# Gate/up feature tiles as seven half products: eight tiles more, raw weights in pairs, evictions in place

## The chip, the cores and the metric

The kernel runs on one core of a Trainium2 chip. The metric is device time in microseconds (us) of one execution. TensorE (PE in the rows, PEld for its weight loads) multiplies, VectorE (DVE) and ScalarE (ACT) do elementwise work, GpSimd (POOL) does a little of it, and SyncE (SP) issues the transfers from HBM. PSUM is the accumulator memory: eight banks of 128 partitions by 512 float32, called B0 to B7 here.

## The reference, cut to what matters

Two layers, each a token mixer (state space heads, stick-breaking attention, block-sparse attention) and a SwiGLU feed-forward part, on 512 tokens of width 1024 in float32. The change lies in the feed-forward part, hidden width 2816:

```
h2 = rms_norm(x, pre_ffn_norm)
f = (jax.nn.silu(h2 @ w_gate) * (h2 @ w_up)) @ w_down
return x + rms_norm(f, post_ffn_norm)
```

`rms_norm(x, w)` is `x * rsqrt(mean(x*x) + 1e-6) * w`, over the width.

## The kernel before, in words

**Two-part numbers.** Every float32 operand of a matmul is split into a high part `hi`, which ScalarE writes (a copy that rounds, L114), and a low part `lo = src - hi`, which VectorE writes (L115). A product is three matmuls: hi by hi, hi by lo, lo by hi (`PASSES`). So each weight tile of 128x1024 costs a transfer of 512 KB by SyncE into a raw slot (`wr0` to `wr2`, a ring of three), a copy of ScalarE into one of four `wh`, and a subtraction of VectorE into one of four `wl`. `chunk` does that for a whole tile (L128 is its transfer).

**The stages of a layer.** Input projections and the mixer; the output projection (L561), in whose end each token tile's post-norm and pre-norm stand (`post_norm` L193 to L197, `pre_norm` L184 to L187, then PE transposes L170 and `to_hT`, which writes the transposed activations hi and lo into `hT` and keeps an unsplit copy, L176); gate/up; down (L685). The stages follow one another with no barrier: the weights of the next stage are fetched and split while the last one multiplies.

**Gate/up.** There are 22 feature tiles of 128 in a layer. Two forms compute one.
- `plain`: gate and up each take 24 matmuls of 128x512 (all 512 tokens; L218 in `fm_mm`): 48. Six tiles, 0, 1, 5, 9, 13 and 17 (`PLAIN`), go this way; 0 and 1 do it by token halves, since the last tokens' norms are still under way.
- `seven`: the other 16. The activations are cut into 2 by 2 blocks (token halves by width halves), and so are the weights: `b11`, `b21` are the two halves of the gate tile, `b12`, `b22` those of the up tile. Seven products of blocks and sums of blocks, in the manner of Strassen and Winograd, take the place of eight: 7 products of 12 matmuls of 128x256 (L619), 84. The sums on the activations' side (`XS`, three in the tiles `D`, one in `RR0` and `RR1`) are made once per layer (L598 to L601). Those on the weights' side are made per tile by VectorE: `t13` holds `b11+b12` and `b12+b22`, `t24` holds `b11+b12+b22` and that plus `b21`; they use `RR2` and `RR3` as scratch.

**A seven tile on the engines.** VectorE does the weight sums (L644, L645, L647, L649), five `lo` subtractions (two of 128x1024, for w0 and w13, and three of 128x512, for the halves of w24 and for w22), and seven operations of 128x256 that combine the products (L658 to L671). ScalarE does the `hi` copies, a copy of the first product out of PSUM (L656) and two silus (L153). The results stand in eight slots `F0` to `F3` (`take_ct`, four per tile), and in the tile `GT[i]`.

**What sets the order.** A scheduler orders each engine's instructions by priorities. The weight work stands under `high_priority(SPLIT_OFF)`, so that it comes ahead of the combining operations where it can. Each engine runs its list strictly in order: an instruction that waits holds all those behind it. A slot of a ring can be filled again only when the last reader of its former content is done.

**Down.** The 22 tiles of `GT` are split into hi and lo again, into the four tiles of `RR` in rotation, hi in one half and lo in the other (`R = cut(RR)`: `RR0` first), and multiplied (L685) into all eight PSUM banks.

## Time and profile before

| | |
|---|---|
| median of 3 runs | 1249.36 us (1248.89 to 1250.68) |
| profiled execution | 1248.79 us; span of its instructions 1247.0 us |
| PE busy | 1214.4 us (97%) |
| DVE, ACT, POOL busy | 825.5 (66%), 590.3 (47%), 54.0 (4%) us |
| granted PE clock, mean over the span | 0.995 of full speed |
| gate/up, layer 0 | 270.12 to 505.51 us (first L218 to first L685) |
| gate/up, layer 1 | 887.11 to 1120.08 us |

Times of rows are in us from the start of the span. The matmuls are pipelined: one of 128x256 is listed with 283 ns, but they start 120 ns apart, so the cost of a matmul is read from a run of them (duration of the run by its count), not from one. The same holds in a smaller way on VectorE and ScalarE, where a next operation can start before the listed end of the last.

### The profile page before, as it was taken

The page shows a single profiled execution, that of the slowest core. Times are in us where ns is not written, and L with a number is a line of the kernel's source. Part 1 is how long each engine was busy: PE and PEld are TensorE (multiplying, and loading weights), DVE is VectorE, ACT ScalarE, POOL GpSimd, SP SyncE. Part 2 cuts the span into 40 slices and gives each one's busy share as a digit, 9 for nine tenths or more (in the row PEclk, how much of TensorE's full clock was granted, in tenths as well). Part 3 has the DMA queues.
Part 4 walks back from the last instruction along what each step waited for, and adds up shares of the span by engine and source line. Part 5 has one row for each costly group of instructions (what it writes and reads, how often), then busy time and mean ns, then how long its engine had stood idle before and what let it go on. Part 6 is the DMA issues. An engine that isn't in the chain of part 4 may idle for free.

```text
span 1247.0 us, 18442 instructions
## 1 busy us (share of the span) xinstructions
PE 1214.4 (97%) x7270; PEld 1074.4 (86%) x7270; DVE 825.5 (66%) x1459; ACT 590.3 (47%) x1084; POOL 54.0 (4%) x88
## 2 busy tenths in 40 slices
PE   6999999999999999899999999999999999999997
PEld 5877888889999999788877888888899999998886
DVE  5466866889777768433465578578897778683334
ACT  5555664465444444422355566635654444353232
POOL 1010000110000000000010100001000000000000
PEclk9999999999999999999999999999999999999999
DMA  7332233242333333333324322221423323334321
GB/s 243 119 96 74 85 102 102 69 152 68 105 116 96 108 102 117 120 101 98 105 85 135 120 70 83 77 94 68 153 70 103 116 92 108 106 107 131 92 77 68
DMA packets 40775, 128.90 MB, mean 103 GB/s; under 512 B 5456, under 2 KB 5744, under 8 KB 40688
## 3 DMA queue, kind: packets, MB, share of 16 engines
q1 hardware_dynamic: 39344, 123.49, 30.9%
q0 software_dynamic: 1344, 4.23, 1.0%
q8 instruction: 57, 0.93, 0.3%
q14 instruction: 30, 0.25, 0.1%
HBM read 123.47 MB, written 4.23 MB: 102 GB/s over the span
## 4 chain that ended last, share of the span: by engine, by line
PE 91%; DVE 3%; ACT 2%; issue 1%; DMA 1%; SPq 0%; DVEq 0%; POOLq 0%; POOL 0%; ACTq 0%
PE B L218 24%; PE B L619 23%; PE B L685 19%; PE B L209 7%; PE B L561 7%; PE B L336 2%; PE B L343 1%; PE B L449 1%; PE B L314 1%; DMA wr<-in_wch_dram 1%; PE B L170 1%; PE B L521 1%; PE B L315 1%; DVE wl L115 1%; ACT wh L114 1%
## 5 line engine op out<-in xcount | busy, mean ns | idle before, releaser
L218 PE MATMUL B<-hT,wh 128*128 128x512 f32 (+1 forms) x1024 | 296.6, 370 | 2.2 <-ACT F L303 2.2
L115 DVE TENSOR_TENSOR wl<-wr,wh 128x1024 fp32r<-128x1024 f32 (+1 forms) x204 | 230.5, 1137 | 84.2 <-ACT wh L114 82.2
L114 ACT ACTIVATE wh<-wr 128x1024 fp32r<-128x1024 f32 (+1 forms) x204 | 200.4, 989 | 129.6 <-DMA wr<-in_wch_dram 40.1
L218 PEld LDWEIGHTS B<-hT,wh 128*128 128x128 f32 x1024 | 184.7, 191 | 31.6 <-ACT F L303 3.3
L685 PE MATMUL B<-wh,RR 128*128 128x512 f32 x704 | 189.8, 389 | 3.9 <-ACT RR L114 3.9
L218 PE MATMUL B<-hT,wl 128*128 128x512 f32 (+1 forms) x512 | 188.2, 369 | 0.0
L685 PEld LDWEIGHTS B<-wh,RR 128*128 128x128 f32 x704 | 132.0, 188 | 31.6 <-ACT RR L114 4.3
L619 PE MATMUL B<-hT,wh 128*128 128x256 f32 x768 | 152.1, 283 | 0.9 <-ACT F L656 0.9
L619 PE MATMUL B<-D,wh 128*128 128x256 f32 x768 | 148.9, 283 | 0.0
L619 PEld LDWEIGHTS B<-hT,wh 128*128 128x128 f32 x768 | 125.5, 192 | 1.5 <-ACT F L656 1.4
L619 PEld LDWEIGHTS B<-D,wh 128*128 128x128 f32 x768 | 123.9, 192 | 0.4
L114 ACT ACTIVATE wh<-RR 128x512 fp32r<-128x512 f32 (+1 forms) x96 | 73.9, 774 | 97.7 <-PE B L619 42.5
L685 PE MATMUL B<-wl,RR 128*128 128x512 f32 x352 | 109.5, 389 | 0.0
L218 PEld LDWEIGHTS B<-hT,wl 128*128 128x128 f32 x512 | 97.7, 191 | 13.7
L619 PE MATMUL B<-hT,wl 128*128 128x256 f32 x384 | 108.7, 283 | 0.0
L619 PE MATMUL B<-D,wl 128*128 128x256 f32 x384 | 107.8, 283 | 0.0
L115 DVE TENSOR_TENSOR RR<-F,RR 128x512 fp32r<-128x512 f32 x48 | 33.1, 691 | 111.3 <-ACT RR L114 110.6
L115 DVE TENSOR_TENSOR wl<-RR,wh 128x512 fp32r<-128x512 f32 (+1 forms) x96 | 82.5, 863 | 17.7 <-ACT wh L114 17.2
L114 ACT ACTIVATE RR<-F 128x512 fp32r<-128x512 f32 x48 | 30.0, 629 | 131.2 <-PE B L685 130.8
L209 PE MATMUL B<-wh,hT 128*128 128x512 f32 x256 | 84.1, 404 | 2.4 <-DVE hT L115 2.4
L685 PEld LDWEIGHTS B<-wl,RR 128*128 128x128 f32 x352 | 66.1, 188 | 13.7
L561 PE MATMUL B<-wh,RR 128*128 128x512 f32 x256 | 77.2, 398 | 0.0
(190 smaller groups left out, 1869.1 us busy)
## 6 DMA issues: line engine op xcount, KB each, us to landing
wr<-in_wch_dram SPq DMA_DIRECT2D x204, 512.0 KB, 3.6
x<-in_x_dram SPq DMA_DIRECT2D x16, 256.0 KB, 3.4
F<-in_gains_dram SPq DMA_DIRECT2D x16, 256.0 KB, 4.1
F<-acd POOLq DMA_DIRECT2D x16, 256.0 KB, 6.2
xsave<-x SPq DMA_DIRECT2D x8, 256.0 KB, 2.1
x<-xsave SPq DMA_DIRECT2D x8, 256.0 KB, 3.4
out_dram<-x SPq DMA_DIRECT2D x8, 256.0 KB, 2.0
D<-in_mixgain_dram SPq DMA_DIRECT2D x4, 256.0 KB, 4.9
```

Of the source, the lines that this page charges most:

```text
L114: A.activation(hi, src, AF.Copy)
L115: return eng.tensor_tensor(lo, src, hi.bitcast(F32), op=OP.subtract)
L170: T.transpose(p[:, i * P:(i + 1) * P], srcs[q + i], ident)
L209: T.matmul(p, hT[a][:, k, t * P:(t + 1) * P], w[k // 2][b][:, (k % 2) * 512:(k % 2 + 1) * 512], start=n == 0, stop=n == 3 * KT - 1)
L218: T.matmul(p[:, t0 * P:t1 * P], w[b][:, k * P:(k + 1) * P], hT[a][:, k, t0 * P:t1 * P], start=first and n == 0, stop=n == 3 * KT - 1, skip ...
L314: T.matmul(p, tiles[2 + h][:, cs], tiles[h][:, cd], start=True, stop=False, skip_group_check=True)
L315: T.matmul(p, tiles[2 + h][:, cs], tiles[4 + h][:, cd], start=False, stop=stop, skip_group_check=True)
L336: T.matmul(pz[:, o:w], ntri if i2 == i else nones, s2, start=False, stop=i2 == NT - 1 and n == 1, skip_group_check=True)
L343: T.matmul(pv[:, j * 64:(j + 1) * 64], e[:, (j - i) * P:(j - i + 1) * P], VT[i][:, h * 64:(h + 1) * 64], start=i == NT - 1, stop=i == 0 an ...
L561: T.matmul(OB[j][hf], lt, w[b][:, hf * 512:(hf + 1) * 512], start=k == ks[0] and a == 0 and b == 0, stop=k == ks[-1] and a == 1)
L619: T.matmul(p, w[b][:, half * 512 + k * P:half * 512 + (k + 1) * P], left(j, a, k), start=first and k == 0 and n == 0, stop=k == 3 and n == ...
L685: T.matmul(B[2 * t + hf], gs[a][:, t * P:(t + 1) * P], w[b][:, hf * 512:(hf + 1) * 512], start=i == 0 and a == 0 and b == 0, stop=i == HT ...
```

## The change

- `PLAIN` becomes `(0, 1)`: tiles 5, 9, 13 and 17 are computed as seven half products too, 20 of 22 in each layer.
- The raw weights lie in one tensor `WRT` of four slots of 128x1024. The first three are the ring of `chunk`. The fourth is also the norms' scratch `F[43:45]`. `seven` takes slots in pairs: 0 and 1, or 2 and 3.
- `t13` is made in one VectorE operation of 128x1024 (L648: `b11` and `b22` by a stride, `b12` broadcast over both) where two of 128x512 stood (L644, L647).
- The products are combined in place: the silus write into their PSUM banks (`pa`, `pd`), the subtraction of `wv` from `pd` as well; the two multiplications read one operand from PSUM. A tile takes two slots of `F0`, `F1`, not four of `F0` to `F3`; the silu of plain tiles uses `F2`, `F3`.
- `to_hT` splits first and keeps the copy after.
- `down` begins its rotation with `RR2` and `RR3`.

Lines move by two to four: L115 becomes L117, L619 L622, L644 L648, L645 L650, L649 L653, L656 L660, L658 to L671 L662 to L675, L685 L689.

```diff
-PLAIN = (0, 1, 5, 9, 13, 17)
+PLAIN = (0, 1)
...
-    WR = [cp.tile([P, D], F32, name=f"wr{i}") for i in range(NRAW)]
+    WRT = cp.tile([P, NRAW + 1, D], F32, name="wr")
+    WR = [WRT[:, i] for i in range(NRAW)]
+    F[43:45] = [WRT[:, NRAW, h * 512:(h + 1) * 512] for h in range(2)]
...
         def dst(q, n, p):
+            sl = slice(t * P, (t + 1) * P)
+            split(p.rearrange("p (k l) -> p k l", k=4), hT[0][:, q:q + n, sl], hT[1][:, q:q + n, sl])
             if keep is not None:
                 A.activation(keep[q // 4], p, AF.Copy)
-            sl = slice(t * P, (t + 1) * P)
-            split(p.rearrange("p (k l) -> p k l", k=4), hT[0][:, q:q + n, sl], hT[1][:, q:q + n, sl])
...
-        take_sg = ring(F[43:45])
-        take_ct = ring([f[:, h * 256:(h + 1) * 256] for f in F[0:4] for h in range(2)])
+        take_sg = ring(F[2:4])
+        take_ct = ring([f[:, h * 256:(h + 1) * 256] for f in F[0:2] for h in range(2)])
+        take_pair = ring([WRT[:, 0:2], WRT[:, 2:4]])
...
-            rg, ru = take_raw(), take_raw()
-            b11, b21, b12, b22 = rg[:, lo5], rg[:, hi5], ru[:, lo5], ru[:, hi5]
-            for n, r in enumerate((rg, ru)):
-                nc.sync.dma_start(r, wch[l, C_GU + 2 * i + n])
+            raw = take_pair()
+            for n in range(2):
+                nc.sync.dma_start(raw[:, n], wch[l, C_GU + 2 * i + n])
+            rg, raw4 = raw[:, 0], raw.rearrange("p a (h n) -> p (a h) n", h=2)
+            b21, b22 = raw4[:, 1], raw4[:, 3]
...
-                V.tensor_tensor(t13[:, lo5], b11, b12, op=OP.add)
+                V.tensor_tensor(t13.rearrange("p (h n) -> p h n", h=2), raw4[:, 0:4:3],
+                                raw4[:, 2:3].to_broadcast([P, 2, 512]), op=OP.add)
                 V.tensor_tensor(t24[:, lo5], t13[:, lo5], b22, op=OP.add)
                 split(t24[:, lo5], w24[0][:, lo5], w24[1][:, lo5])
-                V.tensor_tensor(t13[:, hi5], b12, b22, op=OP.add)
...
-            wv, xv, uv, sg = take_ct(), take_ct(), take_ct(), take_ct()
+            wv, xv = take_ct(), take_ct()
...
-            silu(sg, pa)
+            silu(pa, pa)
             product(pd, w24, 1, 2, False)
-            V.tensor_tensor(uv, pd, wv, op=OP.subtract)
-            silu(uv, uv)
-            V.tensor_tensor(t1, xv, uv, op=OP.mult)
+            V.tensor_tensor(pd, pd, wv, op=OP.subtract)
+            silu(pd, pd)
+            V.tensor_tensor(t1, pd, xv, op=OP.mult)
             product(pc, w22, 0, 6, False)
             V.tensor_tensor(wv, wv, pc, op=OP.subtract)
-            V.tensor_tensor(t0, wv, sg, op=OP.mult)
+            V.tensor_tensor(t0, pa, wv, op=OP.mult)
...
-        R = cut(RR)
+        R = cut(RR[2:4] + RR[0:2])
```

Three places of the program show how instructions move. The number behind a name tells which allocation it is; B0 to B7 are PSUM banks, wl and wh the split weights, wr the raw slots.

**The start of gate/up, layer 0, on VectorE.** L197 or L199 ends a token's post-norm (token tile 3's here), L187 or L189 is the pre-norm of token tiles 2 and 3, L644 or L648 the first weight sum of feature tile 2. Before:

```order
L644 TENSOR_TENSOR RR2_2162<-wr1_107,wr2_108 128x512
L647 TENSOR_TENSOR RR2_2162<-wr2_108 128x512
L197 SCALAR_TENSOR_TENSOR x30_1243<-F2_65,SM_117,x30_1243 128x512
L197 SCALAR_TENSOR_TENSOR x31_1244<-F3_66,SM_117,x31_1244 128x512
L160 TENSOR_SCALAR SM_117<-SM_117 128x1
L645 TENSOR_TENSOR RR3_2163<-RR2_2162,wr2_108 128x512
L160 TENSOR_SCALAR SM_117<-SM_117 128x1
L187 SCALAR_TENSOR_TENSOR F0_63<-x20_1241,SM_117,F20_73 128x512
L187 SCALAR_TENSOR_TENSOR F1_64<-x21_1242,SM_117,F21_74 128x512
L649 TENSOR_TENSOR RR3_2163<-RR3_2163,wr1_107 128x512
L187 SCALAR_TENSOR_TENSOR F43_84<-x30_1243,SM_117,F20_73 128x512
L187 SCALAR_TENSOR_TENSOR F44_85<-x31_1244,SM_117,F21_74 128x512
```

Now the same stretch reads:

```order
L117 TENSOR_TENSOR wl3_112<-wr_104,wh3_108 128x1024
L162 TENSOR_SCALAR SM_113<-SM_113 128x1
L199 SCALAR_TENSOR_TENSOR x30_1239<-F2_65,SM_113,x30_1239 128x512
L199 SCALAR_TENSOR_TENSOR x31_1240<-F3_66,SM_113,x31_1240 128x512
L189 SCALAR_TENSOR_TENSOR F0_63<-x20_1237,SM_113,F20_73 128x512
L189 SCALAR_TENSOR_TENSOR F1_64<-x21_1238,SM_113,F21_74 128x512
L162 TENSOR_SCALAR SM_113<-SM_113 128x1
L648 TENSOR_TENSOR RR2_2158<-wr_104 128x1024
L189 SCALAR_TENSOR_TENSOR wr_104<-x30_1239,SM_113,F20_73 128x512
L189 SCALAR_TENSOR_TENSOR wr_104<-x31_1240,SM_113,F21_74 128x512
L650 TENSOR_TENSOR RR3_2159<-RR2_2158,wr_104 128x512
L117 TENSOR_TENSOR hT1_95<-B1_97,hT0_94 128x4x128
```

The weight sum moved behind token tile 2's pre-norm and stands right ahead of token tile 3's, whose scratch is now the fourth raw slot.

**The steady state of gate/up, layer 0, on VectorE.** Twelve rows in a row, from the weight sum of one tile on. L666, L668, L670 and L671 are the last four combining operations of a tile (L670, L672, L674 and L675 now), L658 to L662 the first three (L662 to L666 now). Before:

```order
L644 TENSOR_TENSOR RR2_2162<-wr1_107,wr2_108 128x512
L647 TENSOR_TENSOR RR2_2162<-wr2_108 128x512
L645 TENSOR_TENSOR RR3_2163<-RR2_2162,wr2_108 128x512
L658 TENSOR_TENSOR F0_63<-B4_102,F0_63 128x256
L649 TENSOR_TENSOR RR3_2163<-RR3_2163,wr1_107 128x512
L660 TENSOR_TENSOR F0_63<-F0_63,B3_101 128x256
L115 TENSOR_TENSOR wl3_116<-RR3_2163,wh3_112 128x512
L662 TENSOR_TENSOR F0_63<-F0_63,B1_99 128x256
L115 TENSOR_TENSOR wl0_113<-RR2_2162,wh0_109 128x1024
L115 TENSOR_TENSOR wl2_115<-wr1_107,wh2_111 128x1024
L666 TENSOR_TENSOR F1_64<-B3_101,F0_63 128x256
L115 TENSOR_TENSOR wl3_116<-RR3_2163,wh3_112 128x512
```

Now:

```order
L117 TENSOR_TENSOR wl2_111<-RR2_2158,wh2_107 128x1024
L117 TENSOR_TENSOR wl0_109<-wr_104,wh0_105 128x1024
L648 TENSOR_TENSOR RR2_2158<-wr_104 128x1024
L670 TENSOR_TENSOR B3_99<-B3_99,F0_63 128x256
L117 TENSOR_TENSOR wl1_110<-RR3_2159,wh1_106 128x512
L650 TENSOR_TENSOR RR3_2159<-RR2_2158,wr_104 128x512
L674 TENSOR_TENSOR F0_63<-F0_63,B1_97 128x256
L117 TENSOR_TENSOR wl3_112<-wr_104,wh3_108 128x512
L672 TENSOR_TENSOR F18_1231<-B3_99,F0_63 128x256
L653 TENSOR_TENSOR RR3_2159<-RR3_2159,wr_104 128x512
L675 TENSOR_TENSOR F18_1231<-B2_98,F0_63 128x256
L117 TENSOR_TENSOR wl1_110<-RR3_2159,wh1_106 128x512
```

L648 takes the place of L644 and L647, and it stands ahead of the last four combining operations of the tile that PE is finishing; those write or read PSUM now (`B3`, `B2`), where `F1` stood.

**The end of gate/up and the start of down, layer 0, on ScalarE.** F12 to F15 are the first four results of gate/up, that down splits into RR; L153 (L155 now) is the silu. Before:

```order
L656 ACTIVATE F2_65<-B5_103 128x256
L114 ACTIVATE wh2_111<-wr1_107 128x1024
L114 ACTIVATE wh0_109<-wr2_108 128x1024
L153 ACTIVATE F3_66<-B5_103 128x256
L114 ACTIVATE wh1_110<-wr0_106 128x1024
L153 ACTIVATE F3_66<-F3_66 128x256
L144 ACT_TABLE_LOAD
L114 ACTIVATE RR0_4380<-F12_67 128x512
L114 ACTIVATE RR1_4381<-F13_68 128x512
```

Now:

```order
L116 ACTIVATE RR2_4574<-F12_67 128x512
L116 ACTIVATE wh1_106<-RR3_2159 128x512
L155 ACTIVATE B3_99<-B3_99 128x256
L116 ACTIVATE wh3_108<-wr_104 128x512
L116 ACTIVATE RR3_4575<-F13_68 128x512
L660 ACTIVATE F1_64<-B5_101 128x256
L116 ACTIVATE wh2_107<-wr_104 128x1024
L116 ACTIVATE wh0_105<-wr_104 128x1024
L155 ACTIVATE B5_101<-B5_101 128x256
L116 ACTIVATE wh1_106<-wr_104 128x1024
L116 ACTIVATE RR0_4572<-F14_69 128x512
L116 ACTIVATE RR1_4573<-F15_70 128x512
```

The split of F12, the first that down's matmuls read, moved from behind the last silu and the table load to the middle of the last feature tile.

## Rows read from the trace of the kernel before

**Rows 1.** Page, section 1: busy us, share of the span, instructions.

```profile
PE 1214.4 (97%) x7270; PEld 1074.4 (86%) x7270; DVE 825.5 (66%) x1459; ACT 590.3 (47%) x1084; POOL 54.0 (4%) x88
```

**Rows 2.** PE's waits, 255 to 630 us: line, releaser: us, times, longest.

```profile
PE B L685 <- ACT RR L114: 3.1, 1, 3.1
...
PE B L170 <- DVE hT L115: 1.6, 1, 1.6
PE B L619 <- ACT F L656: 0.5, 1, 0.5
```

**Rows 3.** PE's waits, 870 to 1247 us (L170 and L619 as in rows 2).

```profile
PE B L685 <- ACT RR L114: 0.8, 1, 0.8
```

**Rows 4.** Chain that ended last: start, us, engine, line, count.

```profile
270.12 11.51 PE B L218 x96
...
409.97 10.95 PE B L218 x48
...
452.60 10.91 PE B L218 x48
463.51 37.45 PE B L619 x312
...
505.51 116.79 PE B L685 x514
...
887.11 11.51 PE B L218 x96
...
1120.08 115.68 PE B L685 x509
```

**Rows 5.** Windows: stretch, length, busy us by engine, clock, DMA share, GB/s.

```profile
463.50:501.00 37.50, 37.50 (x315) 37.50 (x314) 31.39 (x55) 18.21 (x30) 0.00 (x0) 1.00 0.32 99
```

**Rows 6.** DVE by line and form, 255 to 520 us: busy us, mean ns.

```profile
L115 DVE TENSOR_TENSOR wl<-wr,wh 128x1024 fp32r<-128x1024 f32 x38 | 45.9, 1220 | 14.2 <-ACT wh L114 14.0
...
L668 DVE TENSOR_TENSOR F<-F,F 128x256 f32<-128x256 f32 x16 | 6.7, 418 | 0.0
...
L660 DVE TENSOR_TENSOR F<-F,B 128x256 f32<-128x256 f32 x16 | 6.6, 415 | 2.6 <-PE B L619 2.1
```

**Rows 7.** Timeline of DVE, layer 0: start us, us, instruction.

```profile
467.23 0.68 DVE L645 TENSOR_TENSOR RR<-RR,wr 128x512 f32<-128x512 f32 x1
467.84 1.21 DVE L115 TENSOR_TENSOR wl<-wr,wh 128x1024 fp32r<-128x1024 f32 x1
468.97 0.41 DVE L660 TENSOR_TENSOR F<-F,B 128x256 f32<-128x256 f32 x1
469.30 0.68 DVE L649 TENSOR_TENSOR RR<-RR,wr 128x512 f32<-128x512 f32 x1
```

**Rows 8.** ACT by line and form, 255 to 520 us.

```profile
L153 ACT ACTIVATE F<-F 128x256 f32<-128x256 f32 x16 | 6.6, 413 | 4.9 <-DVE F L666 4.9
...
L153 ACT ACTIVATE F<-B 128x256 f32<-128x256 f32 x16 | 5.8, 365 | 0.0
```

**Rows 9.** L639, the transfers of seven tiles: waiters (us, times), landing times.

```profile
  DVE RR L644: 19.4, 24
...
DMA to landing us min/median/max: 3.3/3.6/5.3
```

**Rows 10.** Timeline at the end of gate/up, layer 0.

```profile
499.98 2.01 ACT L114 ACTIVATE wh<-wr 128x1024 fp32r<-128x1024 f32 x2 [3.30 <-DMA wr<-in_wch_dram]
...
504.82 1.15 ACT L114 ACTIVATE RR<-F 128x512 fp32r<-128x512 f32 x2
```

**Rows 11.** Timeline of ACT at the end of gate/up, layer 1.

```profile
1115.98 2.01 ACT L114 ACTIVATE wh<-wr 128x1024 fp32r<-128x1024 f32 x2 [2.36 <-DMA wr<-in_wch_dram]
```

**Rows 12.** Timeline of DVE at the start of gate/up, layer 0.

```profile
280.68 1.41 DVE L187 SCALAR_TENSOR_TENSOR F<-x,SM,F 128x512 f32<-128x512 f32 x2
282.74 0.69 DVE L600 TENSOR_TENSOR F<-F,F 128x512 f32<-128x512 f32 x1 [0.65 <-ACT F L176]
```

More of the change, by code (lines that the diff above doesn't have):

```diff
@@ L71, in cut @@
         return [t[:, h * 512:(h + 1) * 512] for t in tiles for h in range(2)]
-    F = [None if 4 <= i < 12 or 18 <= i < 20 or 28 <= i < 40 else cp.tile([P, 512], F32, name=f"F{i}")
+    F = [None if 4 <= i < 12 or 18 <= i < 20 or 28 <= i < 40 or i >= 43 else cp.tile([P, 512], F32, name=f"F{i}")
          for i in range(NF)]
```

## The prediction

> **What bounds the kernel now.** The page's busy shares come first: PE is busy for 97% of the span, DVE for 66%, ACT for 47% [rows 1]. So nearly all of the time is the matmuls' own, and the kernel can gain in two ways only: fewer or cheaper matmuls, or the few us in which PE waits. PE's waits in the two stretches that the change touches are 3.1 us at down's first matmul in layer 0 and 0.8 us in layer 1, 0.5 us in either layer at the first seven tile, and 1.6 us in the transposes ahead of gate/up [rows 2, 3]. Between those waits the chain that ended last consists of PE runs alone: a plain tile is 48 matmuls in 10.91 to 10.95 us, and 312 matmuls of 128x256 take 37.45 us [rows 4]. The window over that second run shows PE busy for all of its 37.50 us, DVE for 31.39 and ACT for 18.21, with the clock at 1.00 [rows 5]. So in gate/up PE sets the pace, DVE follows at 84%, and what a tile costs is its number of matmuls by their spacing, as long as DVE keeps up.
>
> **The change part by part.**
>
> *Four plain tiles per layer become sevens.* The run of sevens gives 37.45 / 312 = 0.120 us a matmul, so a tile of 84 takes 10.08 us. A plain tile takes 10.93 (the middle of 10.91 and 10.95) [rows 4]. That is 0.85 us less per tile, 6.8 us for eight. It is all on PE's path.
>
> These rows also price size: a 128x512 matmul takes 10.93 / 48 = 0.228 us, two of 128x256 take 0.240, so halving the width costs 5%. The Trainium skill (Perfetto Trace Analysis, Optimizing Tensor Performance, Matmuls) says that larger matmuls are more efficient than smaller ones, which speaks against the change. The rows agree with it, and the 6.8 us has that price in it: by columns alone (84x256 against 48x512, 12.5% fewer) a tile would save 1.37 us, and eight 10.9.
>
> *DVE's work per seven tile.* In the timeline the next operation starts 0.61 us after one of 128x512, 1.13 after one of 128x1024 and 0.33 after one of 128x256 [rows 7]. Before, a tile is two of 1024 columns, seven of 512 and seven of 256: 2x1.13 + 7x0.61 + 7x0.33 = 8.84. With the fused `t13` it is three, five and seven: 3x1.13 + 5x0.61 + 7x0.33 = 8.75. Against PE's 10.08 DVE has 1.33 us free per tile (87% full). Before, plain tiles gave it more rest: they need little of DVE, and a seven behind one could run ahead. Now 20 sevens follow one another, so this 1.33 us has to suffice each time. It does if no single wait in DVE's queue is longer.
>
> *In place in PSUM.* Three of DVE's 256-column operations change where an operand or the result lies: two multiplications read one operand from PSUM, and the subtraction `pd - wv` writes its result there. Reading is shown: 415 ns with a PSUM operand (L660), 418 with both in SBUF (L668) [rows 6]. Writing PSUM from DVE or ACT no row shows. The bounds: nothing, or even a gain, as ACT's silu takes 365 ns when it reads PSUM and 413 when it reads SBUF [rows 8]; and at the other end as much again as the operation (0.42 us for one DVE operation and 0.37 for each of two silus). I take nothing, the nearest rows being L660 and L668. At the upper end DVE would need 8.75 + 0.42 = 9.17 of 10.08, and ACT has half its time free, so PE would not notice.
>
> The Trainium skill gives a fixed cost per DVE operation of about 60 ns on SBUF and 125 ns on PSUM (Perfetto Trace Analysis, Optimizing Scalar/DVE Operations). As an estimate from that page three operations would cost 3 x 65 = 0.2 us more per tile, and the sum would stay as it is, with the free time of DVE down to 1.1 us. L660 against L668 shows no such difference here.
>
> *Raw weights in pairs.* The gate and up tiles of a feature tile now land in one of two pairs instead of three single slots in rotation. A transfer takes 3.6 us from issue to landing (3.3 to 5.3), and DVE's first weight sum waited for one 24 times, 19.4 us in all [rows 9], without PE waiting for it. A pair is free when the last split that reads it (w22's `lo`) is done. Laying the order of DVE, ACT and PE out by the spacings above, layer 0 issues the up transfer of tile i+2 at 2.0 us into a period of 10.08, it lands at 5.6. DVE ends L666 at about 4.85 (it waits for the fourth product of the tile), `wl2` follows ACT's `wh2` until 6.75 and `wl0` ACT's `wh0` until 8.3, where DVE comes to L648: 2.7 us to spare. In layer 1 the order is another, L648 stands ahead of more: the transfer lands at 6.8 and DVE comes to it at 6.9. There PE has some 1.3 us of weights in hand behind it. So up to a landing of 3.6 + 1.3 = 4.9 us costs nothing, and each us above that is lost 1:1 in that tile. Only landings near the slowest seen (5.3) would be felt, at 0.4 us. I take nothing for both layers; if one in five of layer 1's twenty landed that late, 4 x 0.4 = 1.6 us.
>
> *The start.* The first seven is tile 2. Its gate transfer can only be issued when the first pair is free, that is when tile 1's up weights are split. L648 for tile 2 now waits for it, and stands on DVE ahead of token 3's pre-norm, with the transposes and the first matmuls on token 3 behind that. Before, that pre-norm ran from 280.68 to about 282.1 [rows 12]. By the timeline of before tile 1's up split ends at about 276.2, the transfer lands at 276.2 + 3.6 = 279.8, and L648 (1.13) is followed by the pre-norm until 282.3, so 0.2 to 0.3 us late in layer 0. The transposes of token 2 have moved in among tile 1's matmuls, so that PE has work there, and the 0.5 us wait for L656 at the first seven [rows 2, 3] should go. I take 0.6 us gained in layer 0, between -1 (landing at 5.3 instead of 3.6, less 0.7 covered) and 1.1. In layer 1 the same chain is about 0.85 us later at token 3, and tile 3's split of w0 may be late by 0.65: against the 0.5 won I take nothing, between -0.7 and 0.5.
>
> *to_hT.* The copy that is kept follows the split instead of preceding it, so hT is ready some 0.5 us sooner, and the bank is freed at the same time as before, after three operations on two engines. The 1.6 us wait of the transposes for that bank [rows 2] stays. I cost it at nothing.
>
> *The end.* Before, down's first split had to wait for the last product, since RR0 held one of its operands; it also stood on ACT behind two raw copies that had waited 3.30 us for their transfer, the last silu and a table load, and so began at 504.82, with PE's first down matmul at 505.51 [rows 4, 10]. In the new order that split stands in the last feature tile, into RR2, free after the last weight sum. Then the first down weights (ACT `wh0`, DVE `wl0`) are due last, 8.2 to 8.3 us into the 8.64 that PE spends on the last tile after its second product has gone ahead (72 x 0.120): in time. The 3.1 us [rows 2] go. In layer 1 the copy of a down weight, which waited 2.36 us for its transfer before [rows 11], stands on ACT ahead of two splits of the last tile's own weights, so I keep 0.4 of the 0.8 us wait [rows 3]. Gain 3.1 + 0.4 = 3.5, at worst 0 (the down weights are late instead).
>
> **Sum.** 6.8 (pitch) + 3.5 (ends) + 0.6 (start, layer 0) = 10.9 us. Gate/up lasted 505.51 - 270.12 = 235.4 us in layer 0 and 1120.08 - 887.11 = 233.0 in layer 1 [rows 4]; it would be about 228 and 229. The profiled execution took 1248.79, so 1237.9; the median of the runs lies 0.6 above it, which gives 1238.5. I forecast 1238.
>
> **The rivals.**
>
> *Only the spacing is won.* The ends are not: another wait takes the place, for instance the down weights or the first combined bank in which the silu now works in place, and a start loses what was to be gained. Then 1249.36 - 6.8 = 1242.6; with the lower end of both starts too (-1.7), 1244. For it: DMA stands behind both end waits [rows 10, 11], so removing the split's wait may only show the transfer's. Against: the first weights have 0.3 us or more in hand by the order.
>
> *DVE's queue sets the pace (the slower side).* L648 waits for a transfer at the head of DVE's queue; behind it stand the combining operations that free banks, and the splits that PE waits for. With only two pairs a late landing cannot be made up by an earlier issue. Place: layer 1's twenty sevens, where only 1.3 us is in hand. The gain of 10.9 is used up at 0.55 us per tile of that layer, that is a landing of 5.5 us on average; at 6 us, 1.1 x 20 = 22 lost, 1260. For it: 19.4 us of L644 waits already [rows 9], DVE at 87%. Against: the median landing is 3.6, the slowest 5.3, and the load on the transfers stays at that of the seven windows (99 GB/s, share 0.32, [rows 5]), which 20 sevens now have all the time. A milder form, 0.1 to 0.3 us in each of 40 tiles, gives 1242 to 1250.
>
> *The start blocks.* Token 3's pre-norm behind L648 costs 1 to 2 us per layer, with transfers near 5.3: 1240 to 1242.
>
> *The change does not do what it says*: PE keeps its waits of before and sevens are no cheaper in a row of 20 than in rows of 3. Four of before's stretches of three sevens ran with no wait [rows 2, 3], so I give it little; about 1249.
>
> **How the numbers follow.** Forecast (1236 to 1241): 0.58. Spacing only, with or without a blocked start (1241 to 1245): 0.22. A slow DVE queue, mild (1245 to 1252): 0.10; strong (above 1252): 0.06. Better than forecast (under 1236, ends and starts both at their best: 6.8 + 3.9 + 1.6 = 12.3 gives 1237; less only if PE's spacing falls): 0.04. The range that leaves out 2 in 10 at most, with the bounds of the unknown starts and ends in it: 1235 to 1247. A measurement of this kernel tells about 0.2%, 2.5 us, from no change. Below 1246.9 lie the forecast, the spacing case, the better case and a little of the mild queue: 0.86. Within 1246.9 to 1251.9: 0.06. Above: 0.08.
>
> **What would show it.** Right: in the run of L622 a matmul each 0.120 us through 20 tiles with no wait of PE at L622; gate/up of 228 and 229 us; PE's wait at L689 gone in layer 0; DVE about 87% busy in a window of one period; 256-column operations on PSUM at 0.42 us. Wrong: waits of PE at L622 that repeat each period in layer 1, with DVE's L648 waiting for `wr` longer than 1 us each time; a pre-norm of token 3 behind an L648 that waited; a longer time for L670 or L155, which write PSUM; a first L689 that waits for `wh` or `wl` instead of RR.

## The result, and the profile after

The changed kernel takes 1237.09 us (median of 4 runs, 1234.39 to 1240.12); the kernel before, on the same chip, 1249.76 (1248.89 to 1250.68). The ratio is 0.9899 with a 95% interval of 0.9871 to 0.9927: 12.7 us less, 9 to 16 by the interval. The forecast was 1238, with a range of 1235 to 1247. The profiled execution took 1235.31 us, its span 1233.3.

The page's busy shares, in the columns of [rows 1]:

```profile
PE 1205.4 (98%) x7558; PEld 1080.9 (88%) x7558; DVE 870.2 (71%) x1523; ACT 602.8 (49%) x1124; POOL 55.4 (4%) x88
```

There are 288 matmuls more, eight tiles by 36, and PE is busy for 9.0 us less. PE's waits from 255 to 625 us, where [rows 2] had 3.1 us at down's first matmul and 1.6 in the transposes (the 2.2 us at L211, right behind down, stood in the kernel before too, at L209):

```profile
PE B L211 <- DVE hT L117: 2.2, 1, 2.2
PE B L220 <- ACT hT L116: 0.7, 1, 0.7
PE B L622 <- ACT wh L116: 0.4, 1, 0.4
PE B L622 <- ACT F L660: 0.4, 1, 0.4
```

And from 860 to 1235 us, layer 1, where [rows 3] had 0.8 us at down:

```profile
PE B L220 <- ACT hT L116: 0.7, 1, 0.7
PE B L172 <- DVE F L189: 0.4, 1, 0.4
PE B L622 <- DVE wl L117: 0.4, 1, 0.4
PE B L622 <- ACT F L660: 0.2, 1, 0.2
```

Down (L689) waits in neither layer. Apart from L211, what is left stands in the first 45 us of gate/up, except for the wait for `wl` in layer 1, which stands in its last seven (1103 us). The chain of layer 0 has one run of sevens in it, from late in tile 3 on, that nothing interrupts:

```profile
303.60 7.71 PE B L622 x62
...
312.55 184.65 PE B L622 x1536
497.20 116.51 PE B L689 x514
```

184.65 / 1536 = 0.120 us a matmul, as in [rows 4]. A window of one period shows what the other engines do meanwhile (columns as in [rows 5]); DVE is busy for 90% of it:

```profile
352.50:362.60 10.10, 10.10 (x86) 10.10 (x86) 9.10 (x16) 4.95 (x9) 0.00 (x0) 1.00 0.32 106
```

The operations of DVE and ACT whose operands or result moved to PSUM, beside the fused sum (columns as in [rows 6, 8]):

```profile
L648 DVE TENSOR_TENSOR RR<-wr 128x1024 f32<-128x1024 f32 x20 | 24.4, 1220 | 1.5 <-DMA wr<-in_wch_dram 1.5
...
L670 DVE TENSOR_TENSOR B<-B,F 128x256 f32<-128x256 f32 x20 | 8.5, 427 | 1.3 <-PE B L622 1.3
...
L672 DVE TENSOR_TENSOR F<-B,F 128x256 f32<-128x256 f32 x20 | 8.4, 418 | 0.0
```

```profile
L155 ACT ACTIVATE B<-B 128x256 f32<-128x256 f32 x40 | 14.7, 367 | 1.1 <-DVE B L670 1.1
```

DVE writes PSUM in 427 ns, 9 more than SBUF; ACT in 367 from PSUM to PSUM.

**A measure free of the rest of the program.** Runs of this kernel spread over 5.7 us, and at least a part of that comes from elsewhere. In the stages before gate/up, which the change does not touch, PE waits some 1 us at a few places, and in some executions its granted clock then falls for a few us (a row's clock is the mean of its window). Two windows of the kernel before, and the same two of the changed one:

```profile
100.00:104.00 4.00, 2.98 (x8) 2.36 (x9) 2.76 (x4) 3.88 (x10) 0.00 (x0) 0.67 0.42 131
104.00:108.00 4.00, 4.00 (x20) 3.28 (x19) 1.02 (x2) 0.20 (x1) 0.00 (x0) 0.91 0.02 4
```

```profile
100.00:104.00 4.00, 3.30 (x15) 2.66 (x16) 2.73 (x5) 3.71 (x8) 0.00 (x0) 1.00 0.40 131
104.00:108.00 4.00, 4.00 (x26) 3.55 (x25) 1.58 (x6) 1.11 (x5) 0.00 (x0) 1.00 0.01 4
```

28 matmuls against 41 in these 8 us. From the start of either layer to its gate/up stage the profile of before has three such places (about 100, 630 and 718 us), that of after one (708). So the experiments are read by the stage: from the start of the first gate/up matmul to the start of down's last in PE's timeline. For before that is 269.96 to 625.10 and 886.94 to 1239.66, 355.1 and 352.7 us; for after 267.98 to 616.52 and 876.69 to 1225.91, 348.5 and 349.2. The sum of both layers falls from 707.9 to 697.8, by 10.1 us; the predicted sum was 10.9.

### The profile page after: what moved, and what is told of

Same layout as the page of the kernel before. It is cut to its first block, busy times and chain, and to the rows that moved or that the text cites. A ratio compares the mean times of both kernels' runs of the same rounds, so it can differ in the third digit from the quotient of the medians.

```text
span 1233.3 us, 19116 instructions
## 1 busy us (share of the span) xinstructions
PE 1205.4 (98%) x7558; PEld 1080.9 (88%) x7558; DVE 870.2 (71%) x1523; ACT 602.8 (49%) x1124; POOL 55.4 (4%) x88
## 4 chain that ended last, share of the span: by engine, by line
PE 93%; DVE 2%; ACT 2%; issue 1%; DMA 1%; POOL 0%; SPq 0%; DVEq 0%; POOLq 0%; ACTq 0%
PE B L622 32%; PE B L689 19%; PE B L220 17%; PE B L211 7%; PE B L563 7%; PE B L338 2%; PE B L345 1%; PE B L451 1%; PE B L316 1%; PE B L172 1%; PE B L523 1%; PE B L317 1%; PE B L447 1%; ACT wh L116 1%; PE B L365 1%
## 5 line engine op out<-in xcount | busy, mean ns | idle before, releaser
L117 DVE TENSOR_TENSOR wl<-wr,wh 128x1024 fp32r<-128x1024 f32 (+1 forms) x204 | 227.1, 1118 | 80.9 <-ACT wh L116 79.3
L220 PE MATMUL B<-hT,wh 128*128 128x512 f32 (+1 forms) x768 | 215.1, 361 | 3.5 <-ACT F L305 2.2
L622 PE MATMUL B<-hT,wh 128*128 128x256 f32 x960 | 193.3, 283 | 0.6 <-ACT F L660 0.6
L689 PE MATMUL B<-wh,RR 128*128 128x512 f32 x704 | 191.5, 389 | 0.0
L622 PE MATMUL B<-D,wh 128*128 128x256 f32 x960 | 185.6, 284 | 0.5 <-ACT wh L116 0.4
L622 PEld LDWEIGHTS B<-hT,wh 128*128 128x128 f32 x960 | 158.2, 192 | 1.2 <-ACT F L660 1.2
L220 PEld LDWEIGHTS B<-hT,wh 128*128 128x128 f32 x768 | 135.9, 191 | 23.5 <-ACT F L305 3.3
L689 PEld LDWEIGHTS B<-wh,RR 128*128 128x128 f32 x704 | 132.0, 188 | 27.2
L622 PEld LDWEIGHTS B<-D,wh 128*128 128x128 f32 x960 | 154.5, 192 | 1.1 <-ACT wh L116 0.6
L220 PE MATMUL B<-hT,wl 128*128 128x512 f32 (+1 forms) x384 | 137.8, 360 | 0.0
L622 PE MATMUL B<-hT,wl 128*128 128x256 f32 x480 | 136.0, 283 | 0.4 <-DVE wl L117 0.4
L622 PE MATMUL B<-D,wl 128*128 128x256 f32 x480 | 135.5, 283 | 0.0
L117 DVE TENSOR_TENSOR RR<-F,RR 128x512 fp32r<-128x512 f32 x48 | 33.1, 691 | 111.0 <-ACT RR L116 111.0
L689 PE MATMUL B<-wl,RR 128*128 128x512 f32 x352 | 111.2, 389 | 0.0
L117 DVE TENSOR_TENSOR wl<-RR,wh 128x512 fp32r<-128x512 f32 (+1 forms) x120 | 102.3, 865 | 11.1 <-ACT wh L116 9.0
L622 PEld LDWEIGHTS B<-hT,wl 128*128 128x128 f32 x480 | 92.1, 192 | 0.6 <-DVE wl L117 0.6
L622 PEld LDWEIGHTS B<-D,wl 128*128 128x128 f32 x480 | 92.1, 192 | 0.0
L211 PE MATMUL B<-wh,hT 128*128 128x512 f32 x256 | 82.7, 398 | 2.4 <-DVE hT L117 2.4
L220 PEld LDWEIGHTS B<-hT,wl 128*128 128x128 f32 x384 | 73.2, 191 | 8.8
```

What stands on the lines that cost most here:

```text
L117: return eng.tensor_tensor(lo, src, hi.bitcast(F32), op=OP.subtract)
L211: T.matmul(p, hT[a][:, k, t * P:(t + 1) * P], w[k // 2][b][:, (k % 2) * 512:(k % 2 + 1) * 512], start=n == 0, stop=n == 3 * KT - 1)
L220: T.matmul(p[:, t0 * P:t1 * P], w[b][:, k * P:(k + 1) * P], hT[a][:, k, t0 * P:t1 * P], start=first and n == 0, stop=n == 3 * KT - 1, skip ...
L622: T.matmul(p, w[b][:, half * 512 + k * P:half * 512 + (k + 1) * P], left(j, a, k), start=first and k == 0 and n == 0, stop=k == 3 and n == ...
L689: T.matmul(B[2 * t + hf], gs[a][:, t * P:(t + 1) * P], w[b][:, hf * 512:(hf + 1) * 512], start=i == 0 and a == 0 and b == 0, stop=i == HT ...
```

## The experiments

Each ratio is taken against runs of the kernel before from the same round, whose medians lie between 1249.00 and 1250.57 us; the profile of before is the one described above. "Stages" is the sum just described; "start" runs from the first gate/up matmul to the first of a seven, "sevens" from there to the start of the last one.

| run | median us | ratio (95%) | layer 0 | layer 1 | stages |
|---|---|---|---|---|---|
| before | 1249.76 | | 355.1 | 352.7 | 707.9 |
| after | 1237.09 | 0.9899 (0.9871 to 0.9927) | 348.5 | 349.2 | 697.8 |
| e1 plain only | 1243.41 | 0.9935 (0.9920 to 0.9950) | 352.9 | 349.2 | 702.1 |
| e2 all but plain | 1248.22 | 0.9989 (0.9979 to 0.9999) | 353.5 | 355.3 | 708.8 |
| e3 down from RR0 | 1240.42 | 0.9915 (0.9901 to 0.9930) | 349.7 | 349.0 | 698.7 |
| e4 before, RR2 | 1245.13 | 0.9944 (0.9922 to 0.9967) | 351.9 | 351.7 | 703.6 |
| e11 plain and RR2 | 1239.62 | 0.9923 (0.9910 to 0.9936) | 349.5 | 348.4 | 697.8 |
| e12 and split first | 1258.73 | 1.0066 (1.0051 to 1.0081) | 369.2 | 348.2 | 717.3 |
| e17 split first in layer 1 | 1257.65 | 1.0061 (1.0046 to 1.0076) | 349.7 | 368.1 | 717.8 |
| e7 after, copy first | 1237.31 | 0.9901 (0.9885 to 0.9917) | 348.3 | 348.4 | 696.7 |
| e6 after, SBUF evictions | 1242.50 | 0.9940 (0.9928 to 0.9952) | 350.5 | 352.8 | 703.2 |
| e5 after, t13 in two | 1239.20 | 0.9921 (0.9900 to 0.9942) | 350.3 | 348.3 | 698.6 |
| e8 after, late up | 1269.68 | 1.0156 (1.0137 to 1.0175) | 366.4 | 363.4 | 729.8 |
| e13 one plain tile | 1253.34 | 1.0024 (1.0014 to 1.0034) | 357.2 | 356.2 | 713.3 |

**e1, the new sevens alone.** The kernel before with one line changed:

```diff
-PLAIN = (0, 1, 5, 9, 13, 17)
+PLAIN = (0, 1)
```

> The kernel before with PLAIN = (0, 1) and nothing else: 20 sevens per layer, single raw slots, SBUF evictions, down from RR0. Theory (the spacing is the gain, the slots are not needed for it): 8 x 0.85 = 6.8 us less, 3.4 in each gate/up stage (235.4 to 232.0, 233.0 to 229.6), down's first wait stays near 3.1 and 0.8; time 1249.4 - 6.8 = 1242.6. Rival (three single slots cannot feed 20 sevens in a row): PE waits of 0.1 us or more per seven behind the weights, half the gain or less, 1246 or more.

6.8 us of time (1250.18 in this round, less 1243.41). The stages fall by 5.8, but down's matmuls of layer 0 take 120.9 us there, against 119.6 before (505.51 to 625.10): behind the wait at their start the granted clock stands at its lower level (0.50, 1.2 GHz) from 503 to 505 us, which it did not behind the longer wait in the profile of before. Without that 1.3 the gain is 7.1. The stretch of the sevens is 3.0 us shorter in layer 0 and 3.3 in layer 1, which is 6.3 of the 7.1; the other 0.8 is a shorter gap between the last seven and down. The theory holds and the rival falls: three single slots feed 20 sevens in a row. Most of down's first wait stays:

```profile
PE B L685 <- DVE F L666: 2.5, 1, 2.5
```

**e2, everything else.**

```diff
-PLAIN = (0, 1)
+PLAIN = (0, 1, 5, 9, 13, 17)
```

in the changed kernel.

> The changed kernel with the old list of six plain tiles: all other edits, none of the new sevens. Theory: what is left is the ends (3.1 + 0.4) and the start of layer 0 (0.6): about 4 us less than before, 1245.5; PE's wait at down's first matmul under 0.5 in layer 0. Rival (the freed slots and fused sum are the gain, the sevens little): 7 us or more less, 1242.5 or below. Second rival (each of these edits costs DVE or the queue something): 1249 or more.

A miss. Of the 4 us expected 2 are there (0.9989, interval to 0.9999), and the stages are 0.9 longer than before. Down waits no more, but the plain tiles (L220) do, in layer 1 so:

```profile
PE B L220 <- DVE F L674: 1.5, 1, 1.5
PE B L220 <- DVE wl L117: 0.8, 1, 0.8
```

Layer 0's stages are 1.7 us shorter than before, layer 1's 2.6 longer. So the other edits without the sevens are worth next to nothing, and their share is not a constant that could be added: what they save at down is lost at the plain tiles.

**e3 and e4, down's first tiles.** In the changed kernel, and the reverse in the one before:

```diff
-        R = cut(RR[2:4] + RR[0:2])
+        R = cut(RR)
```

> The changed kernel with down's rotation from RR0 again. Theory: down's first split waits for the last product, and PE waits about 3.1 us at down's first matmul in layer 0 and 0.8 in layer 1: gate/up of layer 0 longer by 3, of layer 1 by 0.4, the time 3.4 longer than the changed kernel's. Rival (the end wait of before came from the down weights' transfer and the crowded ACT, which pairs and evictions in place relieved): the wait at the first down matmul stays under 1 us, and the time within 1 us.

> The kernel before with down's rotation from RR2, nothing else. Theory: 3.1 us of wait in layer 0 go and 0.4 in layer 1, 1246. Rival (down's weights, late by their transfer, are next in line): the wait at down's first matmul stays at 1.5 us or more in layer 0, with wh or wl as what it waits for, and the time falls by 1.5 or less.

e4 is as the theory had it: no wait at down in either layer, 4.3 us off the stages (3.3 and 1.0). e3 is not: with RR0 first the changed kernel waits 0.6 us in each layer, not 3.1 and 0.8, as its rival had it, and its stages grow by 0.9 (the time by 3.3, of intervals that overlap):

```profile
PE B L689 <- ACT RR L116: 0.6, 1, 0.6
```

Two things were late at the end of layer 0 before: RR0, and ACT with two copies that came after their transfer [rows 10]. The rotation alone removes the whole wait of 3.1 us (e4), and the other edits with the new sevens remove all but 0.6 of it without the rotation (e3), so the two shares do not add. The new sevens alone take 0.6 off it (e1: 2.5); which of the other edits takes the rest no run isolated.

**e11 and e12, the smallest version.** The kernel before with `PLAIN = (0, 1)` and the rotation from RR2 (e11); with the split first in `to_hT` as well (e12):

```diff
         def dst(q, n, p):
-            if keep is not None:
-                A.activation(keep[q // 4], p, AF.Copy)
             sl = slice(t * P, (t + 1) * P)
             split(...)
+            if keep is not None:
+                A.activation(keep[q // 4], p, AF.Copy)
```

> The kernel before with the two edits that moved most alone: PLAIN = (0, 1) and down's rotation from RR2. Theory (these two are the whole gain, and they add, as one is pitch and the other a wait at the end): the stages from the first gate matmul to down's last are 7.1 + 4.3 = 11.4 us shorter than before in both layers together, where the changed kernel had 10.1; time about 1238.5, within 2 us of the changed kernel. Rival (pairs, the fused sum and evictions in place are what makes 20 sevens run without waits): repeated PE waits at the sevens, 1242 or more.

> The kernel before with PLAIN = (0, 1), down's rotation from RR2, and in to_hT the split ahead of the kept copy. Theory (the kept copy ahead of the split holds the last transposes, PE's 1.6 us wait at them): the stretch from the first gate matmul to the first seven falls from 26.57 to 25.7 us in both layers, 1.7 less than with the two edits alone. Rival (that stretch is shorter in the changed kernel because its first weight sum and transposes stand elsewhere): it stays at 26.5.

e11's stages are those of the changed kernel, 697.8 both: the two edits are the whole gain of the stages, and pairs, fused sum, evictions in place and the order of `to_hT` together move the stages by nothing. The two single gains do not quite add, though: 11.4 us were expected and 10.1 came. Of e1's 7.1, 0.8 is a part of the gap ahead of down, which the rotation cannot win again, and e11 keeps 0.5 us more in that gap of layer 0 than e4 (PE waits 0.3 there for `wh`).

e12 is the largest surprise: 19 us slower than e11, by two moved lines that have no part in the loop. The start falls to 26.0 us in layer 1 and stays at 26.4 in layer 0, where 25.7 was expected of both. All of the loss is in layer 0's sevens, 223.1 us against 202.6. The same window of 22 us in e12 and then in e11:

```profile
398.00:420.00 22.00, 21.24 (x168) 20.23 (x168) 18.80 (x33) 9.51 (x16) 0.00 (x0) 1.00 0.31 96
```

```profile
398.00:420.00 22.00, 22.00 (x185) 22.00 (x185) 19.68 (x36) 10.53 (x17) 0.00 (x0) 1.00 0.30 96
```

PE's busy time hides the loss (97%): a matmul is listed with 283 ns and starts 120 ns after the last, so a gap of up to 160 ns shows as busy. Its count of matmuls tells the loss: 168 against 185. DVE's waits over layer 0 tell why, e12 first, then e11:

```profile
DVE F L666 <- PE B L619: 19.4, 9, 3.0
DVE RR L644 <- DMA wr<-in_wch_dram: 10.1, 10, 2.9
DVE F L670 <- PE B L619: 9.8, 8, 1.8
DVE wl L115 <- ACT wh L114: 2.7, 8, 0.8
```

```profile
DVE RR L644 <- DMA wr<-in_wch_dram: 14.8, 16, 1.5
DVE wl L115 <- ACT wh L114: 3.4, 2, 3.2
DVE F L670 <- PE B L619: 3.2, 5, 1.0
```

The moved copy made the scheduler lay out DVE's list otherwise from there on. e11 ends the combining operations of a tile before the weight sums of the tile after next (L666, wl1, L668, L670, L671, wl3, L644, L647, L645); e12 mixes them, in another way from tile to tile (in one L666, L644, L647, wl1, L668, L645, L670, wl3; in another L666, wl1, L668, L670, L644, L647, L671, wl3), so that the sums stand behind operations that wait for PE. In e12 DVE's waits for PE, for transfers and for ACT come to 42.0 us in layer 0, 2.1 a tile; with 8.84 us of work that is 10.9, more than PE's 10.08. In e11 they are 23 us with the smaller ones, 1.2 a tile, which fits. A piece of e12's chain that ended last shows the loop (start, us, what):

```profile
397.88 1.15 DVE wl L115
...
399.05 3.50 DMA wr<-in_wch_dram
...
402.64 0.69 DVE RR L644
...
405.81 0.60 DVE RR L649
406.41 0.34 DVE F L660
...
406.80 8.55 PE B L619 x69
```

The split frees the raw slot, the transfer starts, the weight sum waits for it, behind the sums stands L660, and PE needs the bank that L660 reads. Later in the list it is PE that DVE waits for.

**e17, is it the list?** e11 with the split first in layer 1 alone. By its list the bad order now stands in layer 1 and the good one in layer 0, though it is layer 1 whose `to_hT` was harmless in e12.

```diff
-            if keep is not None:
+            if keep is not None and LAY[0] == 0:
                 A.activation(keep[q // 4], p, AF.Copy)
             split(...)
+            if keep is not None and LAY[0] == 1:
+                A.activation(keep[q // 4], p, AF.Copy)
```

> The kernel before with PLAIN = (0, 1), down's rotation from RR2, and the split ahead of the kept copy in layer 1 alone. By its list VectorE has in layer 0 the order of the run with the two edits alone (the sum t13 of the tile after next behind all combining operations), and in layer 1 the order of the slow layer 0 (t13 behind uv = pd - wv, a combining operation that waits for PE, then between the rest of them). Theory (this order of VectorE's list makes the loss: the weight sums stand behind operations that wait for PE, and PE waits for the weights): layer 0's sevens take 202.6 us, layer 1's about 222, PE waits at the sevens repeat in layer 1, time 1256 to 1260. Rival (layer 0's own to_hT or its transfers were the cause, not the list): layer 1 stays at 202.5, time 1238 to 1240.

The loss moved with the list: sevens of 203.4 us in layer 0 and 222.5 in layer 1. The largest of DVE's waits in layer 1, in the lines of this file (L670 is the subtraction into `uv`, L666 in e12):

```profile
DVE F L670 <- PE B L623: 17.1, 8, 3.0
```

That the order of the list makes these 19 to 20 us is shown; which of the swaps within it does was not taken apart.

**e7 and e6, the other edits undone one by one in the changed kernel.** e7 puts the kept copy of `to_hT` first again. e6 brings back the four SBUF slots:

```diff
-            wv, xv = take_ct(), take_ct()
+            wv, xv, uv, sg = take_ct(), take_ct(), take_ct(), take_ct()
...
-            silu(pa, pa)
+            silu(sg, pa)
...
-            V.tensor_tensor(pd, pd, wv, op=OP.subtract)
-            silu(pd, pd)
-            V.tensor_tensor(t1, pd, xv, op=OP.mult)
+            V.tensor_tensor(uv, pd, wv, op=OP.subtract)
+            silu(uv, uv)
+            V.tensor_tensor(t1, xv, uv, op=OP.mult)
```

> The changed kernel with the kept copy of to_hT ahead of the split again. Theory (the order in to_hT is worth the start): the stretch from the first gate matmul to the first seven goes from 25.71 back to about 26.6 in layer 0, the time 1 to 2 us longer. Rival: it stays at 25.7, and the order of to_hT is worth nothing.

> The changed kernel with the evictions of before: silus and the subtraction into SBUF slots, four per tile. Theory (operations on PSUM take as long as on SBUF, 415 to 427 ns both): the time within 1 us of the changed kernel's, no repeated waits. Rival (banks that are held by evictions in place make the waits at the sevens of 0.4 us in the changed kernel): these go, 1 us less or more.

e7: the start of layer 0 goes back from 25.7 to 26.5 us as expected, but the sevens then take 202.2 instead of 203.2, and the time is the same (1237.31), where 1 to 2 us more were expected. What the earlier start wins, waits at the first sevens lose. e6 is 5.4 us slower, with sevens of 205.2 and 208.2 us. Its operations do take as long (413 to 420 ns), but the time is not within 1 us, and the waits at the sevens did not go, so theory and rival both miss. Layer 1:

```profile
PE B L622 <- ACT F L660: 1.7, 2, 1.4
```

Evictions in place are worth these 5 us beside pairs and the fused sum; e11 has neither pairs nor evictions in place, and loses nothing. The order of the list may again be the reason, but no run isolated it for e6.

**e8, e5 and e13.** e8 transfers the up tile twice:

```diff
+            nc.sync.dma_start(raw[:, 1], wch[l, C_GU + 2 * i + 1])
```

e5 makes `t13` in two operations again, in the changed kernel's place; e13 is e7 with `PLAIN = (0,)`.

> The changed kernel with the up tile of each seven transferred twice into its slot, the second transfer after the first has landed: weights complete some 3.5 us later, about 7.1 after the issue. VectorE's list has the sum t13 behind wl0 in both layers. Theory (2.7 us in VectorE's queue and over 2 us of split weights on PE's side are in hand): PE waits under 0.2 us per tile, time less than 4 us above the changed kernel's. Rival (the ring of two pairs has no slack beyond the first wait): at least 0.5 us per tile, 20 us or more.

> The changed kernel with t13 in two operations of 128x512. At the start of layer 1 GpSimd's power for token tile 3's post-norm took 2.60 us, beside a split (1.13) and the sum of 1024 columns (1.13) on VectorE. Theory (GpSimd's operation waits until VectorE has no operation with two SBUF inputs under way): VectorE has a small one-input operation after the first half of the sum now, and GpSimd's takes about 2.0 us there. Rival (it is the program's place, code or address): 2.6 again. VectorE has 0.09 us more work per tile: sevens within 1 us of the changed kernel's in either case.

> The changed kernel with the kept copy first in to_hT and PLAIN = (0,): 21 sevens per layer. Theory (the spacing holds for one more tile): 0.85 us per layer less than with two plain tiles, stages of 347.5 us from the first gate matmul to down's last. Rival (tile 1's plain matmuls by token halves were what PE did while the last tokens were normed): the start waits grow by 1 us or more per layer, and the time is the same or longer.

e8 falls on the rival's side: 32.6 us slower than the changed kernel, 219.9 us for layer 0's sevens. One of the worst periods on SyncE's queue and on DVE (`issue` stands for a wait whose releaser the profile does not show; a transfer issued at 409.28 lands about then):

```profile
404.43 0.33 SPq L641 DMA_DIRECT2D wr<-in_wch_dram  x1
409.28 0.33 SPq L642 DMA_DIRECT2D wr<-in_wch_dram  x1
```

```profile
412.98 1.22 DVE L649 TENSOR_TENSOR RR<-wr 128x1024 f32<-128x1024 f32 x1 [3.24 <-issue]
```

The second transfer is issued 4.85 us after the first and the sum starts 3.70 later, 8.55 in all, where 7.1 was expected. DVE waits 3.24 us for it here. Over layer 0 its waits at this sum are:

```profile
DVE RR L649 <- DMA wr<-in_wch_dram: 22.2, 14, 3.5
DVE RR L649 <- issue: 10.2, 4, 3.2
```

That is 32.4 us, 1.6 a tile, and DVE's spare time per tile is 1.33. The error is in the reckoning of slack: what PE has in hand can be spent once, but a wait that recurs must fit into DVE's spare time of every tile. The extra transfers also slow the others (L641 lands in 4.0 us in the median, 3.5 in the changed kernel), a share that no run took apart.

e5: the time, 1239.20, is 2.1 us above the changed kernel's and the stages 0.8; layer 0's sevens take 205.0 us against 203.2, so "within 1 us" misses there. GpSimd's operation is the subject of the last section. In e13 the rival holds: with one plain tile PE has too little to do while the last tokens are normed, and waits for token 3's pre-norm in layer 0:

```profile
PE B L172 <- DVE F L189: 5.1, 1, 5.1
```

No version tried beats the changed kernel by more than the runs spread.

## Why the prediction was right

- **The pitch**, 6.8 us: right in mechanism and price, 0.120 us a matmul through 20 tiles; in e1, where nothing else changed, the sevens' stretch is 6.3 us shorter.
- **The ends**, 3.5 us: right in size. The first down matmul starts 0.12 us after the last seven's in layer 0, against 3.41 before (502.10 to 505.51), and in layer 1 down's first four stand ahead of it: from the last seven's last matmul to down's end PE needs 3.4 and 1.0 us less. Of layer 1's 1.0, 0.6 is lost again in its last seven, which waits for `wl` behind the copy of a down weight (the chain goes from that weight's transfer at 1096.94 over ACT's copy at 1100.38 to the split at 1103.03); this is the loss that the prediction feared there and put at 0.4. That leaves 3.8 us. The cause was told too narrowly: by e3 the rotation removes a wait of 0.6 us per layer in the changed kernel, by e4 all of the wait in the old one.
- **The starts**, 0.6 us in layer 0 and nothing in layer 1: the step that was mis-sized. They cost some 0.5 us. From the first gate/up matmul to the first seven's the changed kernel is 0.85 and 0.2 us faster, but the sevens behind lose to waits about 1.1 us more than before in layer 0 and 0.5 in layer 1. The wait for the first product's copy (L656, now L660), 0.5 us before, was to go: 0.4 and 0.2 are left, and a wait of 0.4 for `wh` joins it in layer 0. In the other direction the transposes' wait of 1.6 us, which was to stay, is gone, and 0.7 at L220 stands in its place; e7, with the kept copy first, has the 1.6 in layer 1 again. So that `to_hT` came to nothing, as forecast, is luck: what it wins at the start is lost at the sevens. GpSimd's 2.60 us operation (below) goes with a late start in layer 1: 26.35 us in the changed kernel and in e6, which have that operation, against 25.94 to 26.02 in e2, e3 and e5, where it took 1.46 to 2.06.
- **Raw weights in pairs**, nothing: right. The layout had DVE reach layer 1's sum 0.1 us after its transfer, with 1.3 us of weights in hand on PE's side. DVE waits there 13 times, 0.8 us at most and 6.0 in all, and no wait of PE stands behind these.
- **Sum**: 10.9 predicted, 10.1 in the stages (6.8 by the price of a matmul, 3.8 at the ends, less 0.5 at the starts). The rest of the 12.7 us of time lies in stages with the same instructions, where the two profiles differ by the clock's dips; the prediction had no term for it, so that the median lies within 1 us of 1238 is in part luck. Whether the change makes the dips rarer, or the runs fell so, is open: the changed kernel and e7 show a mean clock of 0.997 or more in five of ten runs, before in none of the ten runs beside e7, e11 in none of five, but e6 in two of five and e4, which is before with one line changed, in one of four.
- **In place in PSUM**: its price was right, nothing (427 against 418 ns). The Trainium skill's larger fixed cost for PSUM (Perfetto Trace Analysis, Optimizing Scalar/DVE Operations) does not show here: 9 ns for a write, none for a read. That leaving the evictions out costs 5 us (e6) is not a matter of this price.
- **DVE's queue as the bound**: the mechanism of the rival is real, and one moved copy away (e12, e17): 1.0 us a tile in one layer, 20 us, where the rival had 22. It needs no late landing, though: transfers of the usual 3.5 us and waits for PE in an unlucky order of the list do it. The changed kernel's list does not have that order: its sum L648 stands ahead of L670, which waits for PE, not behind it. e17 shows that this can be read before a run. The sentence that DVE keeps up "if no single wait in DVE's queue is longer" than 1.33 us should have said the sum of its waits in a period.

## What to carry to other kernels

Reckon an in-order engine that feeds the bounding one by its work and all its waits in one period: spare time per period, not stock, is what a recurring wait may use, and a list in which the sums stand behind operations that wait for the bounding engine, and ahead of what that engine needs next, can close a loop, as in e12. Read the list itself after any edit, even one far from the loop, since a scheduler can lay out the whole stage anew. Two edits that shorten the same wait do not add, so undo each in the new kernel and do each in the old one before sharing out a gain.

## What the runs showed of the hardware

GpSimd raises 128 numbers to a power in 0.55 us (553 ns, the median over 50 in the changed kernel; the longest is 2595):

```profile
L163 POOL TENSOR_TENSOR SM<-SM,mhalf x50: 544/553/2595, 5.9 to 1227.9; 128x1 f32<-128x1 f32 x40, 128x2 f32<-128x2 f32 x8, 128x4 f32<-128x4 f32 x2
```

The longest, 2.60 us, is the first of the pair in the next row, at the start of layer 1. DVE went through two operations with two SBUF inputs meanwhile:

```profile
881.05 3.11 POOL L163 TENSOR_TENSOR SM<-SM,mhalf 128x1 f32<-128x1 f32 x2 [3.44 <-DVE SM L162]
```

```profile
880.89 1.21 DVE L117 TENSOR_TENSOR wl<-wr,wh 128x1024 fp32r<-128x1024 f32 x1
882.02 1.21 DVE L648 TENSOR_TENSOR RR<-wr 128x1024 f32<-128x1024 f32 x1
883.16 0.20 DVE L162 TENSOR_SCALAR SM<-SM 128x1 f32<-128x1 f32 x1
```

It ended at 883.65, 0.49 us after DVE came to an operation with one input. In e5 the second operation there is half as long, with a one-input operation behind it:

```profile
886.23 2.79 POOL L163 TENSOR_TENSOR SM<-SM,mhalf 128x1 f32<-128x1 f32 x2 [3.44 <-DVE SM L162]
```

```profile
886.08 1.21 DVE L117 TENSOR_TENSOR wl<-wr,wh 128x1024 fp32r<-128x1024 f32 x1
887.21 0.68 DVE L648 TENSOR_TENSOR RR<-wr 128x512 f32<-128x512 f32 x1
887.81 0.20 DVE L162 TENSOR_SCALAR SM<-SM 128x1 f32<-128x1 f32 x1
887.93 0.68 DVE L651 TENSOR_TENSOR RR<-wr 128x512 f32<-128x512 f32 x1
```

GpSimd's first operation took 2.06 us here, where about 2.0 was expected from the hold alone, and ended 0.48 us after the one-input operation began. At the start of layer 0 of the changed kernel, beside a single split, it took 1.46 and ended at the same distance. The Trainium skill (SBUF — State Buffer, SBUF: two separate sides) has VectorE, in an operation with two SBUF inputs, and GpSimd take a shared port pair, which the first to start holds for its whole instruction. The three durations agree with it for VectorE's hold. For GpSimd's they do not: L651, with two SBUF inputs, starts at 887.93 and takes its usual 0.68 us, while GpSimd's operation is listed until 888.29, as far as the profile's times of GpSimd, which are rough, can tell.
